# One layer's output weights split beside six earlier pairs of heads and kept as parts, and half of another layer's low parts on GpSimd

## The chip, the cores and the metric

The kernel runs on one core of one Trainium2 chip. What is compared is device time in microseconds of one execution, the median of several. Below, PE is the matmul engine (TensorE), PEld its weight loads, DVE is VectorE, ACT is ScalarE, POOL is GpSimd, and SP is the engine whose queue issues the DMA transfers.

## The reference

The reference is a two-layer streaming encoder over 1024 prompt frames and 64 sample frames with a cache of 256, model width 1024, all in float32. Cut to what matters here:

```python
# layer 0 (even): two head groups from one projection, joined before one output projection
o_a = softmax_attend(q_a, k_a, v_a, chunk_mask)          # 8 heads, keys and values from a compressed latent
o_b = band_attend(q_b, k_b, v_b, rel_bias)               # 8 heads, own chunk and the 8 before
mix0 = concat(o_a, o_b) @ w_out_ab                       # (tokens, 1024) @ (1024, 1024)
# layer 1 (odd): stick-breaking attention, 16 heads
z = einsum(q, k) * scale;  log_1m = where(mask, log_sigmoid(-z), 0)
tail = cumsum(log_1m, reverse=True) - log_1m
w = where(mask, exp(log_sigmoid(z) + tail), 0)
mix1 = einsum(w, v) @ w_out_c                            # (tokens, 1024) @ (1024, 1024)
# every layer
x = LN(alpha * x + mix);  x = LN(alpha * x + square(relu(x @ w_up)) @ w_down)
```

The change touches how the two output weights, `w_out_ab` and `w_out_c`, are made ready for their matmuls.

## The kernel before, in words

**Numbers in two parts.** A float32 operand X is used as a high part H, which ACT makes with an activation Copy into the matmul's rounded float type (line 152), and a low part L = X - H, which DVE makes with a subtraction (line 153). In the profile L152 and L153 are therefore all the splits of the program. A product is three matmuls (`mm3`, lines 157 to 159): H by H, H of the operand by L of the weight (L158), L of the operand by H of the weight (L159). The change adds one source line near the top, so lines of the kernel after are one higher up to about line 1037 (L153 becomes L154, L729 becomes L730).

**Stages of layer 1.** Projections of one pair of heads (keys, queries, values; nine steps, each a chunk of 384, 384 or 320 tokens) run beside the attention of the pair before (`odd_mixer`). The attention of a pair turns a block of scores into two sigmoids on ACT (lines 722 and 723), scans them on DVE (L729 where the mask's edge lies in the block, L731 elsewhere), multiplies on POOL (L732), transposes on PE (L175), splits the transposed weights (`wt`) and multiplies with V (L796, L798). The scan of a block starts from the last value of the block before it. Projection weights of 128 by 1024 come through `weight()` (lines 180 to 193): a raw tile `wraw` with one buffer, and parts `wH` and `wL` in two buffers that take turns.

**The end of the attention.** Beside the attention of the last pair there is no projection to run. There `out_early` loads the eight blocks of the output weight (128 by 1024 each, 512 KB), splits them, and starts the output projection for the first token tiles, as steps of two column halves of 512. The operand of such a step is the attention's output of seven pairs, read back from memory (`oT_d`, 128 by 7 by 128, the rows "128x896") and split in the same way. The blocks' splits are tied to the progress of the attention by the table `WEIGHTS`, one number for each block: the index of an attention unit that the split may not precede. The steps themselves are tied by `paced`.

**What sets the order.** Each engine works through its instructions in a fixed order. That order is made before the run by a scheduler that plays the program through with its own costs, and honours the ties above. So a change to one tie or one instruction can move many others.

**Layer 0** has the same shape: in its latent attention the softmax's multiply by the inverse sum (`R<-R,inv`, L671) and the fold of two halves of the output (`o<-o,otmp`, L757) are on POOL, and `out_early` runs beside the last latent pair.

Of the kernel before, what the change touches and what calls it, by code (L numbers as in the profile page):

```python
# [7 lines left out]
F32 = mybir.dt.float32  # L8
F32R = mybir.dt.float32r
# [4 lines left out]
P = 128  # L14
D = 1024
# [45 lines left out]
LAST = [[(0, 3), (1, 1), (0, 2), (1, 0), (0, 4), (1, 3), (0, 1), (1, 2), (0, 0)],  # L61
        [(0, 0), (1, 1), (0, 1), (1, 2), (0, 4), (1, 3), (0, 2), (0, 3), (1, 0)]]

WEIGHTS = [[0, 1, 1, 2, 2, 3, 3, 5], [0, 0, 1, 1, 2, 2, 2, 5]]


class Halves:


    def __init__(self, tiles):  # L70
        self.tiles = tiles
# [52 lines left out]
class Net:  # L124
# [3 lines left out]
    def __init__(self, tc, io):  # L128
        self.tc, self.nc, self.io = tc, tc.nc, io
        self.uid = 0  # L130
        self.alt = False
        self.wturn = 0
        self.pool_fold = None


    def pool(self, name, side, bufs=1, **kw):
# [887 lines left out]
    def odd_mixer(self, xres):  # L1024
        nc, io = self.nc, self.io
        bp = self.pool("b1", "left")
        self.order = [(0, 0), (1, 3), (0, 1), (1, 2), (0, 4), (1, 0), (0, 3), (1, 1), (0, 2)]

        self.own = self.tl(bp, [P, 513], "own", 1)
        nc.gpsimd.memset(self.own, 0.0)  # L1030
        nc.gpsimd.tensor_copy(self.own[:, 384:512], self.ident)
        cp = self.pool("c1", "left")
        qkp = [self.pool(f"qk1{i}", "left") for i in range(2)]
        sets = [self.set64(p) for p in qkp]

        def proj(pair):
            return self.heads64(cp, bp, sets[1 - pair % 2], pair, {"q": io["w_cq"], "k": io["w_ck1"], "v": io["w_cv"]},
                                io["cache_skT"], io["cache_sv"], {"k": io["o_skT"], "v": io["o_svT"]}, 0,
                                order=None if pair else (0, 3, 1, 4, 2, 5, 6, 7, 8))

        score, V, steps = proj(0)
        firsts = [st() for st in steps]

        for t, i in zip(self.turned[-2:], (2, 3)):
            self.after(t, firsts[i])
        for pair in range(8):
            heads = [(V, h, (2 * pair + h) * 64) for h in range(2)]

            def row(h, i, kc, nk):
                return self.row_stick(bp, score(h, i), kc, nk)  # L1050

            if pair == 7:
                qkp[1].release()
                self.xpool.release()
                self.out_space(1, "right")
            marks = self.attend(cp, heads, row, 0)
            if pair == 7:
                ws, ys, steps = self.out_early(1, io["w_out1"], xres, marks)
            if pair < 7:
                score, V, steps = proj(pair + 1)  # L1060
            self.paced(steps, marks, 2 if pair < 7 else -3)
        qkp[0].release()
        cp.release()
        bp.release()
        return ws, ys
# [15 lines left out]
    def out_space(self, layer, side):  # L1081
# [5 lines left out]
        for tag in ("wraw", "wH0", "wL0", "wH1", "wL1"):  # L1087
            sl.free.append((self.wp, tag, 2, D))

    def out_early(self, layer, w, xres, marks):  # L1090


        nc, sl = self.nc, self.slots
        ws = {}
        blocks = [k for k in range(KD) if k != self.late]
        for k, i in zip(blocks + [self.late], WEIGHTS[layer]):
            raw = sl.take([D])
            nc.sync.dma_start(raw, w[k * P : (k + 1) * P, :])
            ws[k] = [sl.take([D], F32R) for _ in "HL"]
            self.split(*ws[k], raw, mark=marks[i])  # L1100
            sl.give(raw)
        ys = {}
        lhs = {}

        def step(t, h):
            if h == 0:
                *lhs[t], ys[t] = self.out_operand(t, xres)
                if t == EARLY[layer][-1]:
                    self.ahead = self.out_operand(OUT_ORDER[layer][0], None)
            c = slice(h * 512, h * 512 + 512)  # L1110
            ps = self.ps("d" if layer else "ds")
            first = None
            for i, k in enumerate(blocks):
                m = self.mm3(ps, *(x[:, i, :] for x in lhs[t]), *(x[:, c] for x in ws[k]), i == 0, i == KD - 2)
                first = first or m
            y = ys[t]
            nc.vector.scalar_tensor_tensor(y[:, c], y[:, c], ALPHA, ps, op0=ALU.mult, op1=ALU.add)
            if h:
                for x in lhs[t]:
                    sl.give(x)  # L1120
            return first

        return ws, ys, [lambda a=a: step(*a) for a in ((t, h) for t in EARLY[layer] for h in range(2))]
# [710 lines left out]
```

## Time and profile before

| | before |
|---|---|
| median of 3 runs | 2818.61 us (2818.22 to 2821.95) |
| the profiled execution | 2818.91 us, span 2817.1 us, mean granted PE clock 0.992 |
| PE busy | 2731.1 us (97%) |
| DVE busy | 2159.4 us (77%) |
| ACT busy | 1515.0 us (54%) |
| POOL busy | 760.2 us (27%) |
| pairs of layer 1 with a projection beside them | up to 1960 us of the span |
| last pair of layer 1 with `out_early` | from 1960 us, PE full again from 1990 us |
| `out_early` of layer 0 beside its last latent pair | about 610 to 636 us |

The profiled execution lies 0.3 us above the median and 1.8 us above its own span. A row of the stage table reads: start and end of the stretch, its length, then for PE, PEld, DVE, ACT and POOL the busy time with the number of instructions, the granted PE clock, the share of the DMA engines and their GB/s. A row of the group table reads: line, engine, operation, result and operands with shapes, count, then busy time and mean nanoseconds of one, then the engine's idle time just before such instructions and what ended it.

### The profile page before, as it was taken

The numbers are of one execution on the slowest core, as the hardware profiler recorded it, in microseconds if no ns is written. First come the engines' busy times: TensorE is split into PE (matmuls) and PEld (weight loads), VectorE is DVE, ScalarE is ACT, GpSimd is POOL, SyncE is SP. The second block draws the span as 40 slices with busy tenths as digits, with TensorE's granted clock in tenths as the row PEclk, the third lists the DMA queues.
The fourth block names the chain that finished last, engine by engine and source line by source line (L and its number), as shares of the span: only waits on it lengthen the run. The fifth ranks groups of instructions, "written<-read, shape, count | busy, mean of one in ns | idle before, by whom it ended". The sixth has DMA issues, their size and how long they took to land. (4 is left out here: it accounts for less than half of the span.)

```text
span 2817.1 us, 46994 instructions
## 1 busy us (share of the span) xinstructions
PE 2731.1 (97%) x16931; PEld 2495.5 (89%) x16931; DVE 2159.4 (77%) x3832; ACT 1515.0 (54%) x3106; POOL 760.2 (27%) x883
## 2 busy tenths in 40 slices
PE   9989998999999999999999999999899999999998
PEld 8989997878899998788789999999789999987786
DVE  5336667885867777899977888878887777789998
ACT  4226666883555556333257777777545555543331
POOL 3022323652100002222543433434330000122245
PEclk9999999999999999999999999999999999999999
DMA  6162224434244457443421111111352444664432
GB/s 198 42 171 72 67 83 102 110 102 141 88 138 140 134 168 254 128 151 116 135 81 64 52 52 51 61 51 64 94 167 87 158 144 131 234 194 123 150 125 83
DMA packets 228600, 331.47 MB, mean 118 GB/s; under 512 B 44720, under 2 KB 161104, under 8 KB 228368
## 3 DMA queue, kind: packets, MB, share of 16 engines
q1 hardware_dynamic: 228368, 328.48, 37.1%
q8 instruction: 134, 2.20, 0.3%
q14 instruction: 98, 0.80, 0.1%
HBM read 214.49 MB, written 109.99 MB: 115 GB/s over the span
## 5 line engine op out<-in xcount | busy, mean ns | idle before, releaser
L732 POOL TENSOR_TENSOR G<-G,S 128x384 f32<-128x384 f32 (+4 forms) x200 | 201.1, 1009 | 344.4 <-DVE S L729 126.2
L157 PE MATMUL d<-xH,wH 128*128 128x384 f32 (+1 forms) x784 | 262.7, 335 | 3.2 <-ACT qS L617 2.3
L159 PE MATMUL d<-xH,wL 128*128 128x384 f32 (+1 forms) x784 | 261.8, 334 | 0.0
L158 PE MATMUL d<-xL,wH 128*128 128x384 f32 (+1 forms) x784 | 260.5, 332 | 0.0
L153 DVE TENSOR_TENSOR wtL<-t,wtH 128x512 fp32r<-128x512 f32 (+2 forms) x328 | 197.0, 618 | 45.0 <-ACT wtH L152 36.2
L152 ACT ACTIVATE wtH<-t 128x512 fp32r<-128x512 f32 (+2 forms) x328 | 170.3, 545 | 46.1 <-PE pv L796 20.2
L796 PE MATMUL pv<-wtH,V 128*128 128x256 f32 (+1 forms) x624 | 158.6, 279 | 4.4 <-ACT o L756 2.7
L671 POOL TENSOR_TENSOR R<-R,inv 128x640 f32<-128x640 f32 (+6 forms) x100 | 115.5, 1167 | 172.9 <-DVE inv L670 101.5
L798 PE MATMUL pv<-wtL,V 128*128 128x256 f32 (+1 forms) x624 | 153.4, 287 | 8.1 <-DVE wtL L153 8.1
L157 PEld LDWEIGHTS d<-xH,wH 128*128 128x128 f32 x784 | 148.2, 189 | 7.4 <-ACT qS L617 3.3
L729 DVE TENSOR_TENSOR_SCAN S<-S,own 128x513 f32<-128x513 f32 (+3 forms) x144 | 144.0, 1010 | 12.0 <-ACT S L722 9.7
L152 ACT ACTIVATE wo<-wo 128x1024 fp32r<-128x1024 f32 (+4 forms) x91 | 81.8, 907 | 125.7 <-PE d L158 28.2
L158 PEld LDWEIGHTS d<-xL,wH 128*128 128x128 f32 x784 | 148.0, 189 | 1.3
L159 PEld LDWEIGHTS d<-xH,wL 128*128 128x128 f32 x784 | 148.0, 189 | 1.2
L798 PEld LDWEIGHTS pv<-wtL,V 128*128 128x128 f32 x624 | 119.7, 192 | 11.8 <-DVE wtL L153 10.3
L796 PEld LDWEIGHTS pv<-wtH,V 128*128 128x128 f32 x624 | 119.5, 192 | 9.8 <-ACT o L756 5.6
L175 PE MATMUL t<-ident,G 128*128 128x128 f32 x600 | 103.4, 277 | 14.8 <-POOL S L720 7.2
L664 PE MATMUL s<-kS,qH 128*128 128x384 f32 (+3 forms) x288 | 105.6, 369 | 3.1 <-DVE mx L687 2.1
L722 ACT ACTIVATE S<-s 128x384 f32<-128x384 f32 (+4 forms) x200 | 98.7, 493 | 14.9 <-PE s L664 13.1
L723 ACT ACTIVATE G<-s 128x384 f32<-128x384 f32 (+4 forms) x200 | 99.4, 497 | 0.1
L664 PE MATMUL s<-kS,qL 128*128 128x384 f32 (+3 forms) x288 | 96.6, 337 | 0.0
L203 POOL TENSOR_TENSOR rr<-rv,mhalf 128x1 f32<-128x1 f32 (+1 forms) x54 | 37.8, 703 | 215.9 <-DVE neg L302 140.6
(1845 smaller groups left out, 9881.7 us busy)
## 6 DMA issues: line engine op xcount, KB each, us to landing
wo<-a_d SPq DMA_DIRECT2D x54, 512.0 KB
a_d<-wo SPq DMA_DIRECT2D x32, 544.0 KB
wo<-in_w_dn SPq DMA_DIRECT2D x27, 512.0 KB
sl<-a_d SPq DMA_DIRECT2D x24, 512.0 KB
wo<-in_w_up SPq DMA_DIRECT2D x21, 512.0 KB
a_d<-sl SPq DMA_DIRECT2D x19, 544.0 KB
sl<-in_w_up SPq DMA_DIRECT2D x17, 512.0 KB
xs<-a_d SPq DMA_DIRECT2D x17, 512.0 KB
```

The lines of the kernel that those rows point to most:

```text
L152: self.after(self.nc.scalar.activation(H, src, AF.Copy), mark)
L153: (engine or self.nc.vector).tensor_tensor(L, src, H.bitcast(F32), op=ALU.subtract)
L157: i = mm(out, aH, bH, start=first, stop=False)
L158: mm(out, aH, bL, start=False, stop=False)
L159: mm(out, aL, bH, start=False, stop=last)
L175: return self.nc.tensor.transpose(out, in_, self.ident[:n, :n])
L664: self.nc.tensor.matmul(ps[:, :n], q, k, start=i == 0, stop=i == len(passes) - 1)
L671: nc.gpsimd.tensor_tensor(R[:, :nk], R[:, :nk], inv.to_broadcast([P, nk]), op=ALU.mult)
L729: nc.vector.tensor_tensor_scan(s[r], s[r], own, carry, op0=ALU.mult, op1=ALU.max)
L732: nc.gpsimd.tensor_tensor(G[:, :n], G[:, :n], S[:, 1 : n + 1], op=ALU.mult)
L796: mm(out, v, wH[:, s : s + n], start=bi == 0 and s == 0, stop=False)
L798: mm(out, v, wL[:, s - n : s], start=False, stop=bi == len(banks) - 1 and j == bank[-1][0])
```

## The change

It has two parts.

1. **Layer 1.** During the projections of pairs 2 to 7, at the first value step, one block of the output weight (blocks 0 to 5) is loaded through `weight()` and split on ACT and DVE. The parts of blocks 0 to 4 are stored to memory as they are (two transfers of 512 KB each, at the second value step). The parts of block 5 stay in their buffers. `out_early` then loads the ten stored parts straight into its slots, takes the kept block as it is, and loads and splits only block 6 and the last block as before.
2. **Layer 0.** In `out_early`, the low parts of four of the eight blocks are made on POOL, not on DVE.

```diff
-WEIGHTS = [[0, 1, 1, 2, 2, 3, 3, 5], [0, 0, 1, 1, 2, 2, 2, 5]]
+WEIGHTS = [[0, 1, 1, 2, 2, 3, 3, 5], [None, None, None, None, None, None, 0, 5]]
...
+        def ahead(k, steps):
+            store = None
+            def step(i):
+                nonlocal store
+                mark = steps[i]()
+                if i == 6:
+                    store = self.split_ahead(io["w_out1"], k, k == 5, mark)
+                elif i == 7 and store:
+                    store(mark)
+                return mark
+            return [lambda i=i: step(i) for i in range(9)]
...
             if pair < 7:
                 score, V, steps = proj(pair + 1)
+                if pair:
+                    steps = ahead(pair - 1, steps)
...
+    def split_ahead(self, w, k, keep, mark):
+        nc = self.nc
+        H, L = self.weight(w[k * P : (k + 1) * P, :].unsqueeze(1), [P, 1, D], ready=mark)
+        if keep:
+            self.parts_kept = k, [x.rearrange("p a b -> p (a b)") for x in (H, L)], f"{self.wturn}"
+            return None
+        self.wturn = 1 - self.wturn
+        self.parts_d[k] = self.tc.dram_tile([2, P, D], F32, name=f"wo{k}_d")
+        def store(mark):
+            for i, x in enumerate((H, L)):
+                self.after(nc.sync.dma_start(self.parts_d[k][i].unsqueeze(1), x.bitcast(F32)), mark)
+        return store
...
     def out_early(self, layer, w, xres, marks):
...
-        for k, i in zip(blocks + [self.late], WEIGHTS[layer]):
+        todo = dict(zip(blocks + [self.late], WEIGHTS[layer]))
+        if layer:
+            k, ws[k], turn = self.parts_kept
...
+        order = sorted(todo, key=lambda k: (k == self.late, k in self.parts_d))
+        for n, (k, i) in enumerate((k, todo[k]) for k in order):
+            if k in ws:
+                continue
+            if layer and k in self.parts_d:
+                ws[k] = [sl.take([D], F32R) for _ in "HL"]
+                for j, x in enumerate(ws[k]):
+                    nc.sync.dma_start(x.bitcast(F32), self.parts_d[k][j])
+                continue
             raw = sl.take([D])
             nc.sync.dma_start(raw, w[k * P : (k + 1) * P, :])
             ws[k] = [sl.take([D], F32R) for _ in "HL"]
-            self.split(*ws[k], raw, mark=marks[i])
+            self.split(*ws[k], raw, nc.gpsimd if not layer and n % 2 else None, marks[i])
             sl.give(raw)
```

The order of instructions moves with it, at three places that the prediction speaks of.

**DVE, last pair of layer 1.** The first rows are of the kernel before, from the last value part that a projection leaves (`V`) to the operand's split of the first early step (`128x896`). Between them stand seven weight splits of 128 by 1024 among attention work; some rows of the middle are left out here by taking the two ends.

```order
L153 TENSOR_TENSOR V_16517<-t_23175,V_16517 64x2x64
L153 TENSOR_TENSOR wo_4_4875_23786<-wo_2_4873_23783,wo_3_4874_23785 128x1024
L153 TENSOR_TENSOR wtL_23275<-t_23269,wtH_23274 128x512
...
L153 TENSOR_TENSOR wo_13_4884_23804<-wo_11_4882_23801,wo_12_4883_23803 128x1024
L153 TENSOR_TENSOR wo_16_4887_23810<-wo_14_4885_23807,wo_15_4886_23809 128x1024
L153 TENSOR_TENSOR wtL_23337<-t_23332,wtH_23336 128x384
L760 TENSOR_TENSOR o_23294<-pv_23268,o_23294 64x256
L153 TENSOR_TENSOR wo_19_4890_23816<-wo_17_4888_23813,wo_18_4889_23815 128x1024
L731 SCALAR_TENSOR_TENSOR S_23378<-S_23378,S_23368 128x385
L729 SCALAR_TENSOR_TENSOR S_23431<-S_23431,own_16501 64x321 x2
L153 TENSOR_TENSOR wH_4893_23822<-wo_20_4891_23819,wraw_23821 128x1024
L153 TENSOR_TENSOR wo_2_4897_23831<-wo_2_4897_23831,wo_8_4899_23835 128x896
```

The same end in the changed kernel, on DVE again, is this:

```order
L732 SCALAR_TENSOR_TENSOR S_23552<-S_23552,S_23542 128x513
L154 TENSOR_TENSOR wtL_23502<-t_23497,wtH_23501 128x384
L730 SCALAR_TENSOR_TENSOR S_23618<-S_23618,own_16501 128x385
L732 SCALAR_TENSOR_TENSOR S_23628<-S_23628,S_23618 128x257
L154 TENSOR_TENSOR wtL_23569<-t_23563,wtH_23568 128x512
L154 TENSOR_TENSOR wo_17_4906_23863<-wo_15_4904_23860,wo_16_4905_23862 128x1024
L730 SCALAR_TENSOR_TENSOR S_23638<-S_23638,own_16501 128x385
L154 TENSOR_TENSOR wtL_23582<-t_23576,wtH_23581 128x512
L732 SCALAR_TENSOR_TENSOR S_23648<-S_23648,S_23638 128x385
L154 TENSOR_TENSOR wo_18_4907_23866<-wo_18_4907_23866,wo_20_4909_23870 128x896
```

Five weight splits are gone from this stretch. In their place stand more scans and more low parts of attention weights: 18 rows (one of them doubled) lie between the last `V` row and the operand's split before, 30 rows (one doubled) after.

**SP, one of the six pairs.** The queue of the DMA issues, first of the kernel before, beside the attention of pair 1:

```order
L193 DMA wraw_19240<-in_w_ck 128x1024
L602 DMA kraw_18560<-in_cache_sv 128x2x128
L629 DMA o_skT<-kraw_18446 128x320
L801 DMA oT_d<-o_17894 64x256
L801 DMA oT_d<-o_17944 64x256
L801 DMA oT_d<-o_18027 64x256
L193 DMA wraw_19352<-in_w_cq 128x1024
```

and the same stretch of the changed kernel:

```order
L194 DMA wraw_18598<-in_w_out 128x1024
L603 DMA kraw_18560<-in_cache_sv 128x2x128
L630 DMA o_skT<-kraw_18446 128x320
L802 DMA oT_d<-o_17894 64x256
L802 DMA oT_d<-o_17944 64x256
L802 DMA oT_d<-o_18027 64x256
L194 DMA wraw_19249<-in_w_ck 128x1024
L819 DMA oT_d<-o_18066 64x64 x2
L1124 DMA wo_d<-wH_3764_18599 128x1024
L1124 DMA wo_d<-wL_3765_18600 128x1024
L802 DMA oT_d<-o_18104 64x256
L630 DMA o_svT<-kraw_18589 128x384
```

The block of the output weight takes the place in the queue that the next pair's key weight (`w_ck`) had. The key weight takes the place of the query weight (`w_cq`), and the two stores come behind it.

**POOL, layer 0**, `out_early` beside the last latent pair. Before:

```order
L757 TENSOR_TENSOR o_7927<-o_7927,otmp_7928 64x256
L671 TENSOR_TENSOR Rs_8063<-Rs_8063,inv_8077 128x320
L757 TENSOR_TENSOR o_8010<-o_8010,otmp_8011 64x256
L671 TENSOR_TENSOR R_8109<-R_8109,inv_8125 128x896
L671 TENSOR_TENSOR R_8128<-R_8128,inv_8144 128x1024
```

and after:

```order
L154 TENSOR_TENSOR wo_7_2087_8404<-wo_5_2085_8401,wo_6_2086_8403 128x1024
L154 TENSOR_TENSOR wo_13_2093_8416<-wo_11_2091_8413,wo_12_2092_8415 128x1024
L758 TENSOR_TENSOR o_7927<-o_7927,otmp_7928 64x256
L672 TENSOR_TENSOR Rs_8063<-Rs_8063,inv_8077 128x320
L154 TENSOR_TENSOR wo_19_2099_8428<-wo_17_2097_8425,wo_18_2098_8427 128x1024
L672 TENSOR_TENSOR R_8109<-R_8109,inv_8125 128x896
L672 TENSOR_TENSOR R_8128<-R_8128,inv_8144 128x1024
L758 TENSOR_TENSOR o_8010<-o_8010,otmp_8011 64x256
```

Three weight low parts stand ahead of the multiplies of two large blocks (896 and 1024 wide); the fourth comes six rows later.

More of the change, by code (lines that the diff above doesn't have):

```diff
@@ L133, in __init__ @@
         self.pool_fold = None
+        self.parts_d = {}
     def pool(self, name, side, bufs=1, **kw):
@@ L1039, in proj @@
                                 order=None if pair else (0, 3, 1, 4, 2, 5, 6, 7, 8))
+        self.parts_d = {}
+        def ahead(k, steps):
[9 more added lines that the diff above has]
+            return [lambda i=i: step(i) for i in range(9)]
         score, V, steps = proj(0)
@@ L1095, in out_early @@
         blocks = [k for k in range(KD) if k != self.late]
-        for k, i in zip(blocks + [self.late], WEIGHTS[layer]):
+        todo = dict(zip(blocks + [self.late], WEIGHTS[layer]))
+        if layer:
+            k, ws[k], turn = self.parts_kept
+            for x, n in zip(ws[k], "HL"):
+                slot = next(s for s in sl.free if s[1] == f"w{n}{turn}")
+                sl.free.remove(slot)
+                sl.used[id(x)] = slot, x
+        order = sorted(todo, key=lambda k: (k == self.late, k in self.parts_d))
[7 more added lines that the diff above has]
+                continue
             raw = sl.take([D])
```

## The prediction

> **What bounds the kernel now.** I read the page's first part, then a table of stages, then the groups, waits and time line of the stages that the change touches.
>
> ```profile
> PE 2731.1 (97%) x16931; PEld 2495.5 (89%) x16931; DVE 2159.4 (77%) x3832; ACT 1515.0 (54%) x3106; POOL 760.2 (27%) x883
> 615.00:636.00 21.00, 16.23 (x71) 12.68 (x70) 20.83 (x44) 15.68 (x31) 10.21 (x10) 0.76 0.40 122
> 1500.00:1960.00 460.00, 444.20 (x2993) 427.28 (x2992) 384.56 (x553) 339.87 (x811) 181.28 (x347) 1.00 0.16 50
> 1960.00:1965.00 5.00, 5.00 (x42) 4.80 (x41) 4.02 (x8) 3.95 (x13) 2.01 (x7) 1.00 0.37 118
> 1965.00:1990.00 25.00, 14.35 (x79) 10.99 (x77) 24.95 (x30) 23.59 (x47) 13.88 (x19) 0.86 0.73 243
> 1990.00:2030.00 40.00, 39.91 (x232) 34.82 (x233) 34.65 (x46) 20.18 (x43) 14.70 (x24) 1.00 0.19 56
> ```
>
> PE is busy 97% of the span, so the whole gain that any reordering can bring is the small idle rest. Three stretches of it matter here. In 1965 to 1990, beside the last pair, PE idles 25 - 14.35 = 10.65 us and part of its work runs at a slowed clock (0.86), while DVE is busy 24.95 of 25. In 615 to 636 (layer 0) PE idles 4.77 us at a clock of 0.76, and DVE is busy 20.83 of 21. In 1500 to 1960, the pairs with a projection beside them, PE idles 15.8 us of 460 and DVE has 75 us free. So two ends are bound by DVE, and the pairs by PE. The change takes weight splits from both ends and puts six of them into the pairs.
>
> What DVE does at the end of layer 1, and how PE meets it:
>
> ```profile
> 1959.94 0.31 PE L159 MATMUL d<-xH,wL 128*128 128x320 f32 x1
> 1960.19 0.69 DVE L153 TENSOR_TENSOR wtL<-t,wtH 128x512 fp32r<-128x512 f32 x1 [0.60 <-ACT wtH L152]
> 1970.42 0.26 DVE L153 TENSOR_TENSOR V<-t,V 64x128 fp32r<-64x128 f32 x1
> 1988.39 1.64 DVE L153 TENSOR_TENSOR wo<-wo,wo 128x896 fp32r<-128x896 f32 x1
> 1990.09 0.50 PE L159 MATMUL d<-wo,wo 128*128 128x512 f32 x1 [2.26 <-DVE wo L153]
> L153 DVE TENSOR_TENSOR wo<-wo,wo 128x1024 fp32r<-128x1024 f32 x6 | 8.4, 1420 | 0.0
> ```
>
> The last projection matmul starts at 1959.94. DVE has caught up with its sources just then: at 1960.19 it had idled 0.60 us for a high part. The first matmul that needs the operand's low part starts at 1990.09, after waiting 2.26 us for DVE's split at 1988.39. Between the last V row and that split lie 17.8 us of DVE work without a gap. Seven weight splits in it take 9.6 us: 8.4 (six) and 1.22 (the seventh has another tile name).
>
> **Part 1, the end of layer 1.** Taken alone, five splits less are 5 x 1.42 = 7.1 us, and the idle of 10.65 us would shrink by as much. But the order of DVE shows other work in their place. I price the 30 rows of the changed order by the means of the stage before it:
>
> ```profile
> L153 DVE TENSOR_TENSOR wtL<-t,wtH 128x512 fp32r<-128x512 f32 x82 | 55.1, 683 | 5.8 <-ACT wtH L152 4.8
> L729 DVE TENSOR_TENSOR_SCAN S<-S,own 128x513 f32<-128x513 f32 x42 | 53.4, 1272 | 3.5 <-ACT S L722 2.5 <-POOL S L720 0.4
> L729 DVE TENSOR_TENSOR_SCAN S<-S,own 128x385 f32<-128x385 f32 x42 | 42.7, 1018 | 4.3 <-ACT S L722 3.7
> L731 DVE TENSOR_TENSOR_SCAN S<-S,S 128x385 f32<-128x385 f32 x28 | 36.7, 1311 | 4.4 <-ACT S L722 3.3 <-ACT V L152 0.5
> L153 DVE TENSOR_TENSOR wtL<-t,wtH 128x384 fp32r<-128x384 f32 x62 | 33.9, 547 | 8.2 <-PE pv L798 5.6 <-ACT wtH L152 1.9
> L153 DVE TENSOR_TENSOR wL<-wraw,wH 128x1024 fp32r<-128x1024 f32 x20 | 27.0, 1351 | 11.7 <-ACT wH L152 11.6
> L731 DVE TENSOR_TENSOR_SCAN S<-S,S 128x513 f32<-128x513 f32 x14 | 26.3, 1880 | 3.6 <-ACT S L722 2.7
> L760 DVE TENSOR_TENSOR o<-pv,o 64x256 f32<-64x256 f32 x54 | 22.1, 409 | 14.4 <-ACT o L759 14.0
> L731 DVE TENSOR_TENSOR_SCAN S<-S,S 128x257 f32<-128x257 f32 x14 | 13.5, 962 | 0.7
> L729 DVE TENSOR_TENSOR_SCAN S<-S,own 64x321 f32<-64x321 f32 x14 | 13.4, 961 | 1.7 <-ACT S L722 1.4
> L153 DVE TENSOR_TENSOR V<-t,V 128x384 fp32r<-128x384 f32 x14 | 7.6, 544 | 7.0 <-ACT V L152 6.9
> ```
>
> Two weight splits (2.8 us by the end's own 1.42), ten scans of L729 (3 of 513, 3.8; 5 of 385, 5.1; 2 of 321, 1.9), six more with a carry (3 of 385, 3.9; 2 of 257, 1.9; 1 of 513, 1.9), ten low parts of attention weights (6 of 512, 4.1; 4 of 384, 2.2) and three folds (1.2) make 28.9 us, against 17.8 before: 11 us more. Against that, the rows that stand ahead of V shrink. Before, DVE needed from 1959.94 to 1970.6 to reach the end of the V row (10.7 us). In the changed order several rows of attention have moved ahead of the projection's end; if DVE has caught up there again, three V splits (0.54 for the largest, 1.2 in all), two scans, a fold and a low part remain up to the end of V, 4.4 us. Together 4.4 + 28.9 + 1.6 (the operand's split) = 34.9 us from the last projection matmul to the first that needs the operand's low part, against 30.1.
>
> PE does more in that time. Between the same two matmuls its order holds 116 matmuls before and 150 after. At the 444.20 us for 2993 of the pairs' stage, 34 more are 5.0 us, and that work is done rather than lost. The end is 34.9 - 30.1 = 4.8 us longer with 5.0 us more work done in it, a gain of 0.2: I take **0**. The bounds: with the scans with a carry as they were in the end itself,
>
> ```profile
> L731 DVE TENSOR_TENSOR_SCAN S<-S,S 128x385 f32<-128x385 f32 x1 | 1.0, 1003 | 0.0
> L731 DVE TENSOR_TENSOR_SCAN S<-S,S 128x257 f32<-128x257 f32 x1 | 0.7, 739 | 0.0
> ```
>
> the chain is 3 x 0.31 + 2 x 0.22 = 1.4 us shorter, and slack of DVE at the start could give 1 more; if DVE is one low part and two scans behind (some 3 us) when the projection ends, it is longer. From -2.5 to +3.
>
> Transfers are not what ends the wait, by this estimate: eleven blocks and parts of 0.52 MB (5.8 MB) at 401 GB/s take 14.5 us,
>
> ```profile
> 1970.00:1975.00 5.00, 2.47 (x18) 1.91 (x17) 5.00 (x8) 4.95 (x11) 4.15 (x5) 1.00 1.02 401
> ```
>
> which from 1966 on, when x's room is free, is 1981, some 12 us ahead of the operand's split at 1993 (1959.9 + 4.4 + 28.9). The operand's own load stands behind them on SP's queue and has the same slack.
>
> **Part 1, the pairs.** Each of six pairs gets one more split, 1.06 us on ACT and 1.35 on DVE, and five of them two stores. DVE has 75 us free in this stage, yet in-order engines pass short delays on:
>
> ```profile
> L152 ACT ACTIVATE wH<-wraw 128x1024 fp32r<-128x1024 f32 x20 | 21.2, 1061 | 10.1 <-PE d L158 9.8
> PE pv L798 <- DVE wtL L153: 5.2, 5, 1.1
> PE t L175 <- POOL S L720: 5.0, 8, 1.3
> 1646.83 0.39 PE L798 MATMUL pv<-wtL,V 128*128 128x256 f32 x1 [1.09 <-DVE wtL L153]
> ```
>
> PE waits 5.2 us for low parts and 5.0 us for transposes' sources, which come from DVE's scans through POOL. If the 20 weight splits of this stage cause all of that, one costs 0.5 us; if they cause all 15.8 us of idle, 0.8; if none, 0. Six are 3.0, 4.7 or 0. I take **+3** since the single gaps (1.09 at 1646.83) are about one split long. On SP's queue the block goes ahead of the next key weight and the stores behind it; the key weight's split now has to wait for the stores, because it takes the same buffers. Behind it on ACT wait sigmoids and high parts of the attention. That split stands 24 rows further on in ACT's order, at ACT's pace here (339.87 us for 811) some 10 us of work, 14 with its idle, and a store of 1 MB at 401 GB/s takes 2.6: covered.
>
> **Part 2, layer 0.**
>
> ```profile
> L153 DVE TENSOR_TENSOR wo<-wo,wo 128x1024 fp32r<-128x1024 f32 x6 | 7.3, 1230 | 0.0
> 626.70 4.21 DVE L153 TENSOR_TENSOR wo<-wo,wo 128x896 fp32r<-128x896 f32 x1
> 626.44 3.53 POOL L671 TENSOR_TENSOR R<-R,inv 128x896 f32<-128x896 f32 x2
> 625.75 0.73 POOL L757 TENSOR_TENSOR o<-o,otmp 64x256 f32<-64x256 f32 x1 [6.45 <-issue]
> L153 POOL TENSOR_TENSOR wo<-wo,wo 128x1024 fp32r<-128x1024 f32 x9 | 23.2, 2581 | 85.7 <-ACT wo L152 73.3 <-DMA sl<-a_d 12.4
> ```
>
> DVE, which is full here, loses four splits of 1.23 us: 4.9. POOL gains four of 2.58: 10.3, and has 10.8 us free in this stretch, 6.45 of it in one gap. But DVE and POOL slow each other: the operand's split took 4.21 us beside 3.53 us of POOL, where 128x1024 alone takes 1.23. So I take a quarter of the saving, **-1**; the bounds are the whole saving (-4.9) and a DVE held up for all of POOL's time (10.3 - 4.9 = +5.4).
>
> Here a rule of the Trainium skill speaks against the change. Its page "SBUF — State Buffer", section "SBUF: two separate sides", says that the pair of ports which DVE and GpSimd share is an exclusive lock: a DVE operation with two SBUF inputs and a GpSimd operation that reads SBUF take turns, each for its whole instruction. The row at 626.70 agrees. By the rule a subtraction moved to POOL gives DVE less than it seems; what that gives in time is the third rival.
>
> **Sum.** 2818.9 (the profiled execution) + 0 + 3 - 1 = 2820.9, or 2820.6 from the median. I predict **2820.7 us**.
>
> **The rivals.**
> *The end's gain is realised.* If DVE has worked off the attention rows by the time the projection ends, out of its 75 us of slack, the chain is short by the five splits (7.1 us), and PE's clock does not fall. With layer 0 at -2 and the pairs at +1, 2818.9 - 8 = 2811. For it: five splits are gone and DVE alone is what PE waits for. Against it: the changed order puts 11 us of attention behind V, and DVE takes its rows in that order.
> *The pairs pay more.* Each added split stalls a high part and a low part in turn, 1.1 + 1.3 us as the largest waits above: 6 x 1.2 = 7 us with one, and no gain at the end, 2818.9 + 7 = 2826. It decides where DVE's or ACT's lead over PE is below one split (1.35 us). Against it: for 20 splits that are there now, the two waits come only 13 times, 0.8 us each.
> *POOL holds DVE in layer 0.* If the four splits block DVE for their whole 10.3 us, the operand's split comes 5.4 us later, and PE with it: with the pairs' +3 this is 2827. For it: 626.70. Against it: much of DVE's work there reads PSUM, and POOL has gaps.
>
> **How the numbers follow.** A measurement of this kernel tells about 0.2% (5.6 us) from no change. The forecast has a chance of 0.48, the end's gain 0.27, the pairs 0.16, POOL's hold 0.09. About 0.015 of the forecast lies beyond that bound on each side, so faster 0.29, same 0.45, slower 0.26. The forecast's own range, with half of each term's bound, is 2816 to 2826; to hold 8 in 10 it must reach into both sides: 2809 to 2829.
>
> **What would show it.** Right: DVE still full from the last projection matmul to the operand's split, and that split about 33 us after the matmul; PE's idle in the end within 2 us of 10.65; three microseconds more of PE waits for low parts and transposes in the pairs; low parts on POOL of 2.5 to 3 us in layer 0 with DVE's neighbours stretched. Wrong: the first early matmul within 25 us of the projection's end; a wait of ACT's key weight split for a DMA; PE idle in layer 0 over 8 us.

## The result

The changed kernel takes 2837.65 us (median of 4 runs, 2833.99 to 2843.95), the kernel before 2818.41 in the same comparison (2817.88 to 2821.95). The ratio is 1.0063 with a 95% interval of 1.005 to 1.0076: slower, and outside the predicted range of 2809 to 2829. Timed again beside other kernels it took 2836.34 where before took 2821.54, a ratio of 1.0047 (1.0033 to 1.0061). Two single runs far above all others, 3555.58 us with the operand loaded first and 4446.31 us with the sixth low part alone on POOL, are left out of the medians and ratios below.

### The profile after

The profiled execution is the longest of the four: 2843.95 us, span 2842.2, mean granted clock 0.985 (0.992 before). First the busy times of the page, whose PE time grew by 15 us though the instructions are the same 16931:

```profile
PE 2746.1 (97%) x16931; PEld 2507.9 (88%) x16931; DVE 2157.5 (76%) x3828; ACT 1512.7 (53%) x3106; POOL 778.7 (27%) x887
```

A full matmul of 512 columns follows the one before it every 0.23 us where the granted clock is 1.00, and every 0.43 us where it is 0.50 (in the profile of before, at 637 and at 632 us). So a longer PE time with equal work is time under a lower clock. Of the 25.1 us by which the span grew, 15.0 stand in the profile as PE busy and 10.1 as PE idle. In all traces the granted clock is either 1.00 or 0.50, and but for the fall at the program's end it stays at 0.50 for 3.4 us or a multiple of that.

To find the place of the loss I numbered the 12,606 matmuls of the products (the three lines of `mm3`) by their start. Number n belongs to the same point of the program in both kernels, apart from the short stretches in which products and attention are interleaved in another order. The lag is the start of number n less that of number n in the profile of before. It is worked out from the traces, and the table gives what it gains from stage to stage, in us. The first and third columns hold code that no version here changes: they show what one profile differs from another by chance. So does the second, from -0.4 to +1.1, for the kernels that change layer 1 alone.

| kernel | to 600 | end of layer 0's attention | layer 0's rest | six pairs | last pair, `out_early` | start of the MLP | rest | sum |
|---|---|---|---|---|---|---|---|---|
| the change | +3.7 | +2.7 | +1.2 | +5.1 | +5.5 | +6.0 | +0.8 | +25.0 |
| the change, again | -0.5 | +3.0 | +1.5 | +5.0 | +6.9 | +5.1 | +0.6 | +21.6 |

The points are the first such matmuls behind the 600th, 675th, 1460th, 1940th, 2080th and 2160th us of the profile of before, and the last of all: numbers 1902, 2053, 6462, 8052, 8416, 8872 and 12605, counted from 0. They start at 624.3, 675.1, 1460.0, 1940.1, 2085.9, 2160.0 and 2808.1 us; ahead of number 1902 stand 40 us of attention alone, in which the lags of the kernels in the tables move by 0.2 us at most. At number 8052 the kernels with layer 1 changed have done 26 more matmuls of the attention than before (24 where nothing is stored), so the line between the fifth and the sixth column is not sharp. Drawn at the last projection matmul, where 18 more are done (1.8 us at the pace of such matmuls in before), it would make these two columns 6.5 and 4.1 for the change, 6.4 and 5.5 the second time. Their sum is the same, and no entry of these columns in the tables below moves by more than 2 us. Four places lose: the end of layer 0's attention (part 2), the pairs, the last pair, and the start of layer 1's MLP, which the diff does not touch.

The end of layer 1's attention, as the stage table of the changed kernel has it (columns as before: stretch, length, busy time and count of PE, PEld, DVE, ACT, POOL, then the clock and the DMA):

```profile
1976.00:1991.00 15.00, 10.39 (x62) 8.18 (x61) 13.51 (x20) 11.77 (x30) 10.57 (x12) 0.88 0.93 327
1991.00:2016.00 25.00, 18.21 (x94) 15.19 (x94) 23.45 (x26) 18.14 (x38) 13.38 (x29) 0.80 0.61 192
2016.00:2030.00 14.00, 14.00 (x77) 11.97 (x76) 9.48 (x14) 5.03 (x10) 6.42 (x5) 1.00 0.15 41
```

PE idles 11.4 us of 40 here, at a clock of 0.88 and then 0.80. Before, it idled 10.65 of 25 at 0.86. The steps of the chain, from the time lines of PE and DVE:

```profile
1975.85 0.31 PE L160 MATMUL d<-xH,wL 128*128 128x320 f32 x1
1982.19 0.28 DVE L154 TENSOR_TENSOR V<-t,V 64x128 fp32r<-64x128 f32 x1
1983.96 1.34 DVE L154 TENSOR_TENSOR wo<-wo,wo 128x1024 fp32r<-128x1024 f32 x1 [0.63 <-ACT wo L153]
1985.23 1.88 DVE L730 TENSOR_TENSOR_SCAN S<-S,own 128x513 f32<-128x513 f32 x1
2011.97 0.76 PE L158 MATMUL d<-wo,wo 128*128 128x512 f32 x1
2012.89 1.06 DVE L154 TENSOR_TENSOR wo<-wo,wo 128x896 fp32r<-128x896 f32 x1
2015.39 0.39 PE L160 MATMUL d<-wo,wo 128*128 128x512 f32 x1
```

From the last projection matmul to the operand's split on DVE pass 37.0 us (28.5 before), and to the first matmul that needs the split's result 39.5 us (30.1 before). And the start of the MLP, two stretches of the changed kernel:

```profile
2118.00:2138.00 20.00, 20.00 (x123) 17.30 (x122) 18.58 (x24) 12.43 (x21) 0.00 (x0) 1.00 0.25 78
2138.00:2158.00 20.00, 16.67 (x113) 16.10 (x112) 19.65 (x25) 13.56 (x20) 3.08 (x2) 0.83 0.14 53
```

```profile
2100.00:2120.00 20.00, 20.00 (x132) 17.97 (x131) 20.00 (x28) 11.55 (x18) 3.58 (x1) 1.00 0.23 66
2120.00:2140.00 20.00, 18.32 (x147) 17.92 (x146) 19.24 (x23) 13.42 (x23) 1.70 (x2) 1.00 0.14 54
```

The second fence is the kernel before at about the same point of the program. There 279 matmuls fit into 40 us at full clock; in the change 236, with 3.3 us of idle and then a clock of 0.83.

### The profile page after: what moved, and what is told of

Its sections match the earlier page's. It is cut to its first block, busy times and chain, and to the rows that moved or that the text cites. A ratio compares the mean times of both kernels' runs of the same rounds, so it can differ in the third digit from the quotient of the medians.

```text
span 2842.2 us, 47011 instructions
## 1 busy us (share of the span) xinstructions
PE 2746.1 (97%) x16931; PEld 2507.9 (88%) x16931; DVE 2157.5 (76%) x3828; ACT 1512.7 (53%) x3106; POOL 778.7 (27%) x887
## 5 line engine op out<-in xcount | busy, mean ns | idle before, releaser
L733 POOL TENSOR_TENSOR G<-G,S 128x384 f32<-128x384 f32 (+4 forms) x200 | 208.2, 1044 | 347.9 <-DVE S L730 162.5
L176 PEld LDWEIGHTS t<-ident,G 128*128 128x128 f32 x600 | 73.5, 143 | 29.9 <-POOL S L721 11.9
L732 DVE TENSOR_TENSOR_SCAN S<-S,S 128x385 f32<-128x385 f32 (+1 forms) x64 | 87.6, 1369 | 15.0 <-issue 5.0
```

Source lines behind the costliest of these rows:

```text
L176: return self.nc.tensor.transpose(out, in_, self.ident[:n, :n])
L733: nc.gpsimd.tensor_tensor(G[:, :n], G[:, :n], S[:, 1 : n + 1], op=ALU.mult)
```

## The experiments

Four theories stood against each other at first; E to H come with their runs. **A**: POOL's part in layer 0 costs. **B**: the added splits beside the pairs cost. **C**: the early operand's load stands behind the transfers of the parts, so the order puts attention ahead of the early steps, and the last pair pays. **D**: the parts take other slots than the raw blocks did, so later work waits for other users of them. All comparisons below are of five rounds, and each set of runs has its own time of before: 2820.86 us for the first four, 2820.46 for the next four, 2821.54 for the last three.

### Each part alone

Part 2 alone takes the kernel before and adds only this (the other run leaves it out of the change):

```diff
-            self.split(*ws[k], raw, mark=marks[i])
+            self.split(*ws[k], raw, nc.gpsimd if not layer and n % 2 else None, marks[i])
```

> Only the second part of the change: in layer 0 every second weight's low part on GpSimd; layer 1 as before. In the profiles of before and of the change the lag of PE grows by 2.7 us across this place (3.73 at the 600th us, 6.45 at the 675th). Theory A (POOL's four splits hold DVE and the latent pair's rows behind them): about 2821, +2 to +4. Rival (the 2.7 us are run-to-run drift, as the 3.7 us ahead of it must be): within 1 us of before, 2818. My blind term for this part was -1.

> Only the first part of the change: blocks 0 to 5 split beside six pairs; layer 0 as before. If the two parts add up and theory A of the run before holds, this has the change's time less 3: about 2831 to 2835. If nearly all of the loss is in layer 0 or in drift, 2819 to 2822. My blind sum for this part was +3.

Part 2 alone took 2822.72 us, a ratio of 1.0006 (0.9997 to 1.0014), not to be told from before. Part 1 alone took 2832.81, 1.0042 (1.0028 to 1.0056). So part 1 makes most of the loss: +12 us of the change's 15 to 19. The profile of part 2 alone still shows the same +2.8 us at its place as the change does, which its timing, +1.9 us, allows but does not prove.

| kernel | to 600 | end of layer 0's attention | layer 0's rest | six pairs | last pair, `out_early` | start of the MLP | rest | sum |
|---|---|---|---|---|---|---|---|---|
| part 2 alone | -0.4 | +2.8 | +1.6 | +0.8 | -0.2 | -0.4 | +0.3 | +4.6 |
| part 1 alone | -0.8 | +1.1 | +1.5 | +1.8 | +4.1 | +4.1 | -0.9 | +10.9 |

Part 1 alone lost +1.8 in the pairs, where the change lost +5.1 and +5.0. The waits are the same, but not the clock. The stage table of the change has this around two waits of 1.47 and 0.92 us and behind them,

```profile
1864.00:1870.00 6.00, 3.37 (x20) 2.46 (x19) 5.77 (x12) 5.00 (x15) 1.36 (x4) 0.83 0.29 105
1870.00:1874.00 4.00, 4.00 (x17) 4.00 (x17) 3.22 (x5) 2.44 (x6) 2.68 (x3) 0.50 0.22 61
```

and that of part 1 alone has this at the same two:

```profile
1858.00:1864.00 6.00, 3.22 (x22) 2.41 (x22) 5.77 (x12) 5.01 (x15) 1.37 (x4) 1.00 0.23 79
1864.00:1868.00 4.00, 4.00 (x27) 3.97 (x26) 3.29 (x6) 3.12 (x8) 2.70 (x3) 1.00 0.21 61
```

17 matmuls in 4 us against 27. One execution dropped to half the clock in a cluster of waits, the other did not. Eight profiles, of kernels below too, have this pair of waits, equal to 0.02 us. How long the clock was at 0.50 there goes with the loss in the pairs:

| time at 0.50 there | kernels | lag gained in the six pairs |
|---|---|---|
| none | part 1 alone; operand first; both mended | +1.8, +2.0, +2.9 |
| 3.4 us | slots as before; slots and operand | +3.1, +3.5 |
| 6.8 us | the change, twice; parts unread, stored | +5.1, +5.0, +4.2 |

### The pairs' work alone

In both kernels layer 0 is as before. In the first all six blocks are split and stored beside the pairs, but `out_early` loads and splits its eight blocks as before. It does work that is never read. The second also leaves the stores out.

```diff
-WEIGHTS = [[0, 1, 1, 2, 2, 3, 3, 5], [None, None, None, None, None, None, 0, 5]]
+WEIGHTS = [[0, 1, 1, 2, 2, 3, 3, 5], [0, 0, 1, 1, 2, 2, 2, 5]]
...
-                    store = self.split_ahead(io["w_out1"], k, k == 5, mark)
+                    store = self.split_ahead(io["w_out1"], k, False, mark)
...
-            if layer and k in self.parts_d:
+            if False:
```

> The six splits are made beside the pairs and stored as parts, all six, but nobody reads them: the last pair loads and splits its eight blocks as the kernel before does. This prices the added work of the pairs alone, with the old end. Theory B (the pairs pay the loss: six splits of 1.1 us on ACT and 1.35 on DVE and 6 MB of stores in in-order engines): 2825 to 2830, nearly the whole loss. Theory C (the loss arises in the last pair, where ten loads of parts stand ahead of the operand): 2819 to 2823, since its first early step stands 79 matmuls after the last projection matmul in PE's order (107 before, 139 in the change).

> As the run with unread parts, but nothing is stored: six blocks are loaded and split beside the pairs and dropped. Theory G (the splits in the in-order rows of ACT and DVE are what the pairs pay): as with the stores, +3 to +5 us. Theory H (the stores hold the key weight's split back): +0 to +2 us.

With stores it took 2825.0 us, 1.0014 (1.0003 to 1.0024); without, 2823.51, 1.0013 (1.0004 to 1.0022). So six splits beside the pairs cost 3 to 4 us, and the stores nothing that the timing shows. That favours theory G over H; the interval without stores (+1.1 to +6.2 us) still holds the upper half of H's +0 to +2. Theory B, as nearly the whole loss, falls. 2825.0 is the lower edge of its band as written, but before itself took 2820.86 here and not the 2818.4 from which the bands were made. As differences, +4.1 lies in C's (+1 to +5) and not in B's (+7 to +12), and 8 us of part 1's loss remain for the last pair and what follows.

What PE waits for in the pairs of the kernel with unread parts, to be read beside the two waits of before (5.2 for low parts, 5.0 for transposes' sources):

```profile
PE t L176 <- POOL S L721: 6.8, 6, 3.0
PE pv L799 <- DVE wtL L154: 3.2, 4, 1.1
PE d L158 <- ACT kraw L628: 3.1, 4, 1.2
```

The longest single wait is 3.0 us, where before it was 1.3. ACT's copies of a projection are waited for as long as before: 3.1 us, then 2.3 for the queries' and 0.8 for the keys' and values'. The low parts' waits are shorter in sum. The wait of 3.0 us comes last, behind number 8052, so it falls into the sixth column of the tables. The kernel without stores, whose order is another, has no such wait; whether that is due to the stores stays open. Up to the last projection matmul PE idles 1.2 us more than before with the stores and 0.2 less without.

### The operand loaded first

Part 1 alone, with the operand and residual of the first early tile loaded ahead of all weights:

```diff
+        early = self.out_load(EARLY[layer][0], xres) if layer else None
         order = sorted(todo, key=lambda k: (k == self.late, k in self.parts_d))
...
-                *lhs[t], ys[t] = self.out_operand(t, xres)
+                *lhs[t], ys[t] = self.out_operand(t, xres, early if t == EARLY[layer][0] else None)
```

> The first part of the change, with one thing moved: the first early operand and its residual are loaded ahead of the weights' parts, not behind the eleven transfers. In the order the operand's split then is the 2nd row behind the last V part on DVE (31st in the change) and the first early matmul stands 66 matmuls after the last projection matmul (139 in the change). Theory C (the operand behind the parts' transfers made the order put attention ahead, and that cost the end): 6 to 10 us less than the first part as it is, about 2822 to 2826. Theory B (the pairs pay): no more than 2 us less.

It took 2822.73 us, 1.0012 (1.0001 to 1.0022), 10.1 us less than part 1 alone in the same set by the medians and 8.5 by the ratios. That is what theory C expected. But the operand and the residual also take their slots ahead of the parts now, so the edit moves the parts' slots too, and no run here moves the load alone. Its stage table from the last projection matmul on:

```profile
1962.00:1977.00 15.00, 10.34 (x64) 8.22 (x63) 13.27 (x19) 12.85 (x31) 10.25 (x12) 0.91 0.89 314
1977.00:1992.00 15.00, 14.46 (x69) 12.42 (x69) 11.76 (x16) 8.14 (x18) 9.75 (x16) 0.75 0.88 298
1992.00:2012.00 20.00, 20.00 (x119) 17.43 (x118) 18.12 (x24) 13.68 (x29) 10.96 (x17) 1.00 0.18 55
```

and its first early matmul, behind a last projection matmul at 1962.18:

```profile
1979.03 0.77 PE L158 MATMUL d<-wo,wo 128*128 128x512 f32 x1
```

It starts 16.9 us after the last projection matmul (36.1 in the change, 26.2 before). PE idles 5.2 us instead of 11.4, since the early products fill it while DVE works off the attention. The clock is still low for a while (0.75).

### The slots as before

The next two kernels give each pair of parts the same slots that a raw block and its parts had, by taking one more and giving it back unused: one with the loads of part 1 alone, one with the operand first.

```diff
             if layer and k in self.parts_d:
+                spare = sl.take([D])
                 ws[k] = [sl.take([D], F32R) for _ in "HL"]
+                sl.give(spare)
```

> The first part of the change with its loads as they are, but each pair of parts takes its two slots as before: one raw slot is taken ahead and given back unused. So the slots, and with them the work that later tiles wait for, are as in the kernel before. In the order the early matmuls of four blocks then stand 68 matmuls after the last projection matmul (139 in the change) and DVE's rows at the start of the MLP stand nearly as before. Theory D (which slots the parts land in makes two losses, 4.5 us in the last pair and 4 us at the start of the MLP, in the profile of the first part alone): about 2822 to 2825, 8 to 11 less than the first part alone. Rival (the operand's place behind the loads is what counts): the last pair's loss stays, 2828 to 2830.

> Operand loaded first and the slots taken as before, both. The operand alone left +5 us at the start of the MLP in its profile (-3.7 us against before at its 2080th us, +1.3 at the 2140th). Theory D: these 4 to 5 us go, 2818 to 2820, about 1 to 3 us under the kernel before. If the loss at the start of the MLP comes from earlier early steps and not from slots: 2824 as with the operand alone.

They took 2821.04 us, 1.0000 (0.9991 to 1.0009), and 2821.6 us, 0.9999 (0.9989 to 1.0008). Either takes the whole loss of part 1 away.

| kernel | to 600 | end of layer 0's attention | layer 0's rest | six pairs | last pair, `out_early` | start of the MLP | rest | sum |
|---|---|---|---|---|---|---|---|---|
| part 1, operand first | -0.8 | -0.3 | -0.4 | +2.0 | -4.3 | +5.0 | +0.7 | +2.0 |
| part 1, slots as before | +1.0 | -0.4 | +2.1 | +3.1 | -6.7 | +4.3 | -0.8 | +2.6 |
| both | -1.1 | +0.7 | +2.6 | +3.5 | -3.4 | -0.6 | +0.8 | +2.6 |
| parts unread, stored | -2.2 | +0.2 | -0.2 | +4.2 | +2.5 | -0.6 | 0.0 | +3.8 |
| parts unread, not stored | -0.6 | 0.0 | -0.2 | +2.7 | -0.2 | +0.1 | +0.3 | +1.9 |

The slots alone were meant to spare both places, and did so only at the last pair. But they did it by the way of theory C: in this kernel's order the first operand has got a slot in a buffer of the projections' weights, and its load stands ahead of the parts on SP's queue,

```
L1185 DMA wL_4912_23871<-oT_d 128x7x128
L630 DMA o_svT<-kraw_23223 128x320
L1153 DMA wo_2_4891_23834<-in_w_out 128x1024
L1150 DMA wo_6_4895_23841<-wo_d 128x1024
```

whereas in the change it is in a slot of `out_early`'s own and stands behind the ten parts and both raw blocks. The three kernels above with the operand early gain 3.4 to 6.7 us in the last pair; both profiles of the change and that of part 1 alone, with the operand late, lose 4.1 to 6.9. PE's idle time from the last projection matmul to the 2087th us (number 8419) tells them apart as clearly: 8.6 to 10.7 us in the four profiles with layer 1 as it was, 11.1 to 11.5 with the operand late, 4.9 to 5.6 with it early. That the load's place made these orders is inferred and was not looked into in the order's maker.

At the start of the MLP theory D holds where both are set (-0.6), and not with the slots alone (+4.3). PE's waits there, first of the change, then of the kernel before, then of the kernel with both:

```profile
PE t L176 <- DVE sl L306: 3.3, 2, 2.2
PE t L176 <- ACT sl L240: 1.2, 1, 1.2
```

```profile
PE t L175 <- DVE sl L305: 1.7, 2, 1.4
```

```profile
PE t L176 <- DVE sl L306: 1.6, 1, 1.6
```

These are transposes of the last normalised tiles, behind a full DVE. In the five profiles with a loss here (the change twice, part 1 alone, operand first, slots as before) the clock then falls to 0.50, for 3.4 or 6.8 us; in the other eight, the kernel before among them, it does not. Which order DVE gets there differs from version to version, with what the order's maker believes to be ready; which belief makes it worse stays open.

### Part 2 in pieces

Two smaller doses in layer 0 alone: the second and fourth block's low parts on POOL, and the sixth block's only.

```diff
-            self.split(*ws[k], raw, nc.gpsimd if not layer and n % 2 else None, marks[i])
+            self.split(*ws[k], raw, nc.gpsimd if not layer and n in (1, 3) else None, marks[i])
```

> Only layer 0, and only two of the eight low parts (second and fourth) on GpSimd; the one that stood ahead of the two large multiplies of the inverse sum (896 and 1024 wide) stays on DVE. Theory E (a split on GpSimd ahead of those multiplies makes the transposes behind them wait, 2.8 us in the profile of the second part alone, and with the operand's split beside them 3.2 us): without it the loss is below 1 us, or a gain of up to 1. Theory F (any GpSimd split takes DVE's time in full): half of the second part's loss, +1.

> Only layer 0, and only one low part (the sixth, the one that stands ahead of the two large multiplies) on GpSimd; all others on DVE. Theory E (this one split starts the chain: POOL runs it and the two multiplies without a gap, and the operand's split on DVE, 5.49 us in the second part's profile, gets in only behind them): no gain over before, +0 to +3 us, though it takes 1.2 us off DVE. Theory F (each split on GpSimd costs or gains the same): about half of what two early ones gave, -2.

Two early ones took 2816.22 us, 0.9988 (0.9979 to 0.9996): faster by 3.4 us as the ratio has it. The sixth alone took 2821.68, 1.0001 (0.9992 to 1.001): nothing gained. Theory F had the wrong sign for the two early ones; its -2 for the sixth is just inside the interval (-2.3 to +2.8 us). E's number holds for the sixth; for the two early ones it expected a gain of no more than 1 us.

Part 2 as it was made (its own profile, layer 1 as before):

```profile
622.49 2.37 POOL L153 TENSOR_TENSOR wo<-wo,wo 128x1024 fp32r<-128x1024 f32 x1
624.82 3.52 POOL L671 TENSOR_TENSOR R<-R,inv 128x896 f32<-128x896 f32 x2
628.31 1.57 POOL L757 TENSOR_TENSOR o<-o,otmp 64x256 f32<-64x256 f32 x1
```

```profile
623.80 5.49 DVE L153 TENSOR_TENSOR wo<-wo,wo 128x896 fp32r<-128x896 f32 x1
```

```profile
622.57 0.90 PE L175 MATMUL t<-ident,Rs 128*128 128x128 f32 x3 [2.83 <-POOL Rs L671]
629.35 0.79 PE L159 MATMUL d<-wo,wo 128*128 128x512 f32 x1 [3.15 <-DVE wo L153]
```

DVE came to the operand's split at 623.80, 2.9 us earlier than before: three of the four splits had stood ahead of it and were gone (the fourth comes later). But POOL's split and the two multiplies followed each other without a gap until 628.3, and the split on DVE ended 1.0 us after that, at 629.29. PE waited for it, and already before that for a small multiply (`Rs`) that stood behind two of POOL's splits. Yet the operand's split ended 1.6 us earlier than in the kernel before (626.70 + 4.21 = 630.91). There PE had work while it waited, products of the attention 64 columns wide and transposes of `R`; in the order with part 2 these stand behind the early products. The stage table, before and with part 2:

```profile
625.00:636.00 11.00, 10.33 (x42) 8.53 (x41) 10.83 (x24) 5.75 (x13) 8.51 (x8) 0.58 0.20 62
625.00:636.00 11.00, 7.76 (x21) 6.15 (x22) 7.87 (x14) 6.37 (x16) 9.90 (x7) 0.54 0.16 54
```

PE idles 3.2 us here where it idled 0.7. How much of the 2.8 us is POOL's hold and how much is the other order of PE was not separated. With two early splits the wait for `Rs` is the same, 2.83 us, but the operand's split comes into a gap of POOL:

```profile
624.89 1.07 DVE L153 TENSOR_TENSOR wo<-wo,wo 128x896 fp32r<-128x896 f32 x1
626.95 5.84 DVE L153 TENSOR_TENSOR wo<-wo,wraw 128x896 fp32r<-128x896 f32 x1
```

It takes 1.07 us, and the next operand's split takes the 5.84, where PE has work (its profile gains 1.6 us at this place). In the kernel with the sixth alone the operand's split is not held (1.73 us at 628.31); there it is another block's low part on DVE, 2.99 us beside POOL's 2.35, and behind it on DVE a maximum that PE waits 2.7 us for:

```profile
621.35 2.35 POOL L153 TENSOR_TENSOR wo<-wo,wo 128x1024 fp32r<-128x1024 f32 x1 [1.08 <-ACT wo L152]
```

```profile
621.79 2.99 DVE L153 TENSOR_TENSOR wo<-wo,wo 128x1024 fp32r<-128x1024 f32 x1
```

So theory E had the right price for the sixth alone by luck, from a chain that did not occur. What the traces show to count is which DVE subtraction starts while POOL runs, and what PE has to do meanwhile.

### Both mended

> The change itself once more, beside the two runs below. If the two parts add up, +12 (first part alone) and +2 (second alone): 2834 to 2836 where before is 2820.5. If they strengthen each other: 2838 as in its first runs.

> Layer 1 with operand first and slots as before, and in layer 0 only the second and fourth low part on GpSimd. If the parts add up: +1 and -4, 2816 to 2818. If the pairs' cost of 3 to 5 us eats it: not below the two early low parts alone (2816.2).

The change again: 2836.34 us, +14.8 on before, as the sum of its parts has it. Layer 1 with operand first and slots as before, with two early low parts on POOL in layer 0: 2818.64 us, 0.9991 (0.9982 to 1.0000). It is not below the two low parts alone (0.9988). As a difference, -2.5 us by the ratio (-5.1 to 0.0), it allows the sum of the parts as well. Of all versions the kernel before with these two low parts is the only one whose interval lies below 1, by 0.12%, and it was timed in one set alone. The split ahead, with both faults mended, pays in the pairs about what it gains at the end: +2.9 and -4.1 us in this kernel's profile.

## Why the prediction was wrong

**The end of layer 1 (my 0, bounds -2.5 to +3).** The reading was right that the five splits gone would be made up for by attention put ahead: 37.0 us to the operand's split, where I had 33.3. The term was mis-sized. I priced DVE's rows as a chain without a gap and at the pairs' means. Measured, the stretch up to the end of the last V row took 6.6 us (I had 4.4, with two scans where four stand), and the rows from there 30.4 (28.9), with some scans stretched (one of 513 took 1.88 us, where I took 1.27) and with 1.9 us of waits for ACT. PE lost 4.1 to 6.9 us by the three profiles, above my bound. Little of that loss is idle time: from the last projection matmul to number 8419 PE idled 11.5 us in the change and 10.7 before, but it ran at half the clock for 13.7 us where it had been 6.8. I had counted the work of that time as done and left out at which clock. I also called the operand's load covered because it would land some 12 us ahead of its split. It did not delay the split on the chip: it was issued at 1988.65, and ACT made the high part at 2007.57, waiting for no transfer. But with that load and its tile's residual ahead of the transfers (twelve of them, I had counted eleven) the order changed on all engines, and 8 to 10 us came back. That the order's maker put the early steps late because of it fits this and was not looked into further. I had shown the two orders and asked only what they cost, not what had made them.

**The start of the MLP (no term).** +4 to +6 us in the profiles of the change and of part 1 alone. I followed the order to the first early step and took PE to be full from there, as it was before from 1990 on. The diff changes which slots tiles take, and with them the order beyond that point. This term was missing from the sum. In the three profiles it is 2.4 to 3.1 us of idle time and 1.7 to 3.4 us for the clock. Operand and slots together took it away; why is argued and not shown.

**The clock (no term).** I wrote that the whole gain of any reordering is PE's small idle rest, and priced idle time alone. Of the 25.1 us that the change's profile is longer, 15.0 are more busy time of PE for the same work, that is, work at half the clock. So one of my signs of being right came true while the time was far off: PE's idle time in the end stayed within 2 us of 10.65. Where DVE is what PE waits for, a part of these 15 us would be idle time at full clock; how large a part is not known.

**The pairs (my +3).** The size came out: +3 to +4 us timed, with the stores, which I had called covered, or without. The reason did not. I expected three more microseconds of waits for low parts and transposes. By the profiles PE idles 1.3 us more up to the last projection matmul in part 1 alone and 1.5 in the change, and the rest of the loss goes with the clock, which a cluster of waits can take down for some microseconds: +1.8 to +2.9 without that, +4.2 to +5.1 with 6.8 us of it. So the number was in part luck.

**Layer 0 (my -1, bounds -4.9 to +5.4).** The sign was wrong, by a little: +2.8 us in the profiles, 1.9 us timed with an interval that holds zero. The third rival had the mechanism in part: POOL held DVE's split of the operand, but that split still ended 1.6 us earlier than before, and not 5.4 later. The Trainium skill's page "SBUF — State Buffer", section "SBUF: two separate sides", has the two engines' shared ports as a lock held for the whole instruction; the trace agrees, in the 5.49 us of an operation that takes 1.07 in a gap. PE's loss came from two waits, 2.83 us for POOL's own multiply behind its splits and 3.15 for the operand, with PE's other work put elsewhere. My quarter of the saving was a mean over a thing that goes by place: two low parts early gain, one in the wrong place gains nothing.

**The rivals.** "The end's gain is realised" (2811) did not come even with the faults mended: 3.4 to 6.7 us at the end, as the lags have it, against 7 predicted, and the pairs' cost against it. "The pairs pay more" (2826) and "POOL holds DVE" (2827) each had a part. I let the cases exclude each other; the costs came together, 3 + 5 + 5 + 2 us, and the range ended at what one of them alone would give.

## What to carry to other kernels

When work is moved and a scheduler makes the order, compare the two orders to the end of the program, not to the first step that interests, and ask of each late row which input was believed late: here one tile's loads moved ahead of a queue of others were worth 8 to 10 us. A split moved to an emptier engine is priced by the place at which it runs: beside whom, and what of the busy engine starts meanwhile. Idle time alone does not price a change on PE: its time at a lower clock belongs to the sum. Where several independent costs are in doubt, let the range hold their sum.

## What the runs showed of the hardware

- A DVE subtraction with both inputs in SBUF that starts while POOL runs such an operation waits, and the profile shows the wait as its duration: 1.07 us in a gap, 4.21, 5.49 and 5.84 beside runs of POOL. These three ended 0.9 to 1.0 us after the last of the multiplies on POOL. A subtraction with one input in PSUM (`wtL` of 128 by 384) took 0.55 us beside the same kind of POOL operation, and 0.54 elsewhere. POOL's fold of 64 by 256 is stretched in the same way (0.73 us in before, 1.57 behind such a subtraction).
- The granted clock fell to 0.50 in a cluster of waits of 1.47 and 0.92 us in five profiles, for 3.4 or 6.8 us, and stayed at 1.00 in three others with the same waits. In the 6 us around one such fall PE was busy for 3.37 us, and its longest wait was 1.47 us.
- Stretches whose code no version changes differ by up to 4 us from the profile of before (the columns "to 600" and "layer 0's rest"), and runs of the kernel before lay between 2814.7 and 2826.4 us. A term of 2 us can't be read from one profile's whole time. The lag across its own place does better where the place is short: 75 us of unchanged code moved it by -0.4 to +1.1.
